# Gated recurrence: the score block of a chunk's own keys takes all 128 keys of the tile as its stationary operand

## The chip, the cores and the metric

One core of a Trainium2 chip runs the whole program. The time of a kernel is the device time of one execution in microseconds (us); the kernel before took 1293.85 us, the median of 3 runs.

## The reference

The program is one inference step of a two-layer trunk (width 1024) over 128 context tokens and 1024 latent tokens. The even layer joins a bidirectional gated linear recurrence (4 heads, state 128x128) and a neighbourhood attention; the odd layer is a convolution with a gated recurrence of its own. Only the first recurrence is touched. Per head and direction it is computed in chunks:

```python
b = jnp.cumsum(log_f, axis=3)
q_dec = q * jnp.exp(b)
k_inv = k * jnp.exp(-b)
att = jnp.where(lower, jnp.einsum('bhntd,bhnsd->bhnts', q_dec, k_inv), 0.0)
o_intra = jnp.einsum('bhnts,bhnsv->bhntv', att, v)
...
o_inter = jnp.einsum('bhntd,nbhdv->bhntv', q_dec, s_prev)
```

So each chunk needs a block of scores: its queries against its own keys, masked to a triangle. The second direction runs over the flipped sequence.

## The kernel before

All 1152 tokens lie on the free axis in three pieces of 384 columns (c = 0, 1, 2), features on the 128 partitions. A piece holds three tiles of 128 tokens (r = 0, 1, 2), and a tile two chunks of 64 tokens (e = 0, 1). Direction d = 0 runs forward, d = 1 backward.

The function att(h, d) makes the scores of one head in one direction, all in float32. For each piece it takes one bank of PSUM (ps_a; there are two) and fills, for each tile, a square of 128 keys (partitions) by 128 queries (columns). The 64 query columns of a chunk are one matmul:

- The chunk that comes first in the direction (e == f, line 561) sees only keys of its own. The stationary operand is the 64 columns of those keys in HK (named kp in the trace), the output is a block of 64 partitions by 64 columns.
- The chunk that comes second (line 563) sees both chunks' keys. Its stationary operand is all 128 key columns of the tile in HA (named s in the trace), the output is 128 partitions by 64 columns.

The moving operand q is 128x64 in both (named eb for d = 0 and q for d = 1). For d = 0 line 561 comes ahead of line 563 in each tile, for d = 1 behind it, so the two lines take turns. A float32 matmul is issued as two pairs of a weight load and a matmul, so line 561 has 4 heads x 2 directions x 9 tiles = 72 matmuls and 144 instructions of each kind, and so has line 563; a line-561 matmul with its line-563 neighbour is called a pair here, and there are 72.

The scores leave PSUM by three reads for each piece: two masked copies on DVE (line 566, the two diagonal blocks of 64x64) and one copy on ACT (line 569, recorded at line 77 of the helper act: the block of the second chunk's queries with the first chunk's keys). The fourth block, the first chunk's queries with the second chunk's keys, is read by nobody.

Around att, ew1, ew1x and ew2 prepare a head (scans on DVE, exponentials on ACT, products on DVE and POOL), ew3 and ktrans follow it, kv makes the chunk states, o_chunk the outputs (bank ps_o, of which there is one) and o_trans transposes them. These are put on an agenda and run between the units of the big input projections: unit_f (lines 316 to 318) and unit_v (lines 339 to 341), 24 matmuls each. Weights are loaded on the SP queue, split into a high part on ACT (wh, line 77) and a low part on POOL (wl, line 186), one to three blocks ahead. The framework orders each engine's instructions by priority, operands and free buffers when the program is built, and sets the semaphores; on the chip each engine goes through its list in that order.

Of the kernel before, what the change touches and what calls it, by code (L numbers as in the profile page):

```python
# [33 lines left out]
def trunk_kernel(ctx: ExitStack, tc: tile.TileContext, x, wm0, wm, bmr, wfe, wv, woe, wfo, woo, rgw, sm, st0,  # L34
# [7 lines left out]
    V, A, G, PE = nc.vector, nc.scalar, nc.gpsimd, nc.tensor  # L42
# [4 lines left out]
    def slab(name, shape=(128, T), dt=F32):  # L47
        return sp.tile(list(shape), dt, name=name, tag="slab")
# [3 lines left out]
    def psum(tag, shape=(128, 512)):  # L52
        return pp.tile(list(shape), F32, name="ps_" + tag, tag=tag, bufs=PB[tag])
# [15 lines left out]
    def act(out, in_, func, **kw):  # L69

        if func in SETS and chain["set"] not in SETS[func]:
            ld = mybir.InstLoadActFuncSet(name=nc.get_next_instruction_name(), engine=nc.scalar.engine,
                                          act_func_set_id=SETS[func][0], ins=[], outs=[])
            nc.scalar.add_instruction(ld)
            after(ld, chain["users"])
            chain.update(load=ld.name, set=SETS[func][0], users=[])
        i = A.activation(out, in_, func, **kw)  # L77
        if func in SETS:
            after(i.ins, [chain["load"]])
            chain["users"].append(i.ins.name)  # L80
        return i
# [238 lines left out]
    def unit_f(i, c, tag=None):  # L320

        ucount[0] += 1
        ps = psum(tag or ("o" if i >= IFO and ucount[0] % 4 == 0 else "mm"))
        o = ps[:, :CW]
        for k in range(8):
            mm_f(o, i, c, k)
        return o
# [30 lines left out]
    HQ, HS, HK = {}, {}, {}  # L358
# [49 lines left out]
    for jj in range(4):  # L408
        pm = psum("a")
        for kk in range(4):  # L410
            for k in (2 * kk, 2 * kk + 1):
                for b in range(4):
                    PE.matmul(pm[32 * b:32 * b + 32, 0:128], condS[:, k, :],
                              rows[jj, kk][:, (k % 2) * 512 + b * 128:(k % 2) * 512 + (b + 1) * 128],
                              start=(k == 0), stop=(k == 7), skip_group_check=True)
# [126 lines left out]
    def qt(h, d, c, r, n=128):  # L542
        if d == 0:
            return HC[h, 0][:, c * CW + r * n:c * CW + (r + 1) * n]
        return HQ[h, c][:, r * n:(r + 1) * n]

    def att(h, d):

        t = slab("at", (128, 9, 128))
        HAT[h, d] = t  # L550
        f, a = d, HA[h, d]
        fs, gs = slice(64 * f, 64 * f + 64), slice(64 - 64 * f, 128 - 64 * f)
        for c in range(3):
            pa = psum("a")
            for r in range(3):
                o = pa[:, r * 128:(r + 1) * 128]
                z = slice(r * 128, (r + 1) * 128)
                for e in range(2):
                    q = qt(h, d, c, 2 * r + e, 64)
                    if e == f:  # L560
                        PE.matmul(o[fs, fs], HK[h, d, c][:, z][:, fs], q, start=True, stop=True)
                    else:
                        PE.matmul(o[:, gs], a[:, c * CW + r * 128:c * CW + (r + 1) * 128], q, start=True, stop=True)
            p3 = pa[:, :CW].rearrange("p (t s) -> p t s", s=128)
            for zs in (fs, gs):
                V.tensor_tensor(t[zs, 3 * c:3 * c + 3, zs].bitcast(I32), p3[zs, :, zs].bitcast(I32),
                                am[zs, None, 128 * d + zs.start:128 * d + zs.stop].to_broadcast([64, 3, 64]),
                                OP.bitwise_and)
            act(HAT[h, 0][fs, 3 * c:3 * c + 3, gs], p3[fs, :, gs], AF.Copy)
        for c in range(3):  # L570
            HK.pop((h, d, c))
        if d == 1:
            t0 = HAT[h, 0]
            t1 = HAT.pop((h, 1))
            for zs in (fs, gs):
                G.tensor_tensor(t0[zs, :, zs], t0[zs, :, zs], t1[zs, :, zs], OP.add)
# [92 lines left out]
    def head(h, first=None):  # L669
        i0 = IH[h]  # L670
        U = clock["u"] + (15 if h == 0 else 12)
        at(U, s0_load, h)
        for d in range(2):
            at(U + STEP[0], ew1, h, d)
        for d in range(2):
            at(U + STEP[1], ew1x, h, d)
        for d in range(2):
            for n, f in enumerate((ew2, att, ew3, ktrans)):
                at(U + STEP[2 + n], f, h, d)
            at(U + STEP[6], kv, h, d, 0)  # L680
            at(U + STEP[7], kv, h, d, 1)
        for c in range(3):
            at(U + STEP[8 + c], o_chunk, h, c)
            at(U + STEP[8 + c], o_done, h, c)
            at(U + STEP[11 + c], o_trans, h, c)
        for n in range(4):
            w_get(i0 + n, 0, 2)
            for c in range((2 if n < 3 else 1) if first else 0, 3):
                o = unit_f(i0 + n, c)
                with tc.high_priority(200):  # L690
                    head_evac(h, n, c, o)
                tick()
            split.pop(i0 + n)
# [226 lines left out]
    for p in range(4):  # L920
        for n in range(3):
# [5 lines left out]
            for c in range(3):  # L927
                o = unit_f(i, c, (None, "a", "b")[c] if p == 3 and n == 2 else None)
                tick()
                z = slice(c * CW, (c + 1) * CW)  # L930
# [85 lines left out]
    for t in range(9):  # L1016
# [10 lines left out]
        if t in HT1:  # L1027
            c = HT1.index(t)
# [188 lines left out]
    for pos in range(max(ev) + 1):  # L1217
# [6 lines left out]
        n, c = seq[pos]  # L1224
# [147 lines left out]
```

## Time and profile before

| | us |
|---|---|
| median of 3 runs | 1293.85 |
| the 3 runs | 1293.85, 1298.67, 1292.9 |
| the profiled execution | 1299.53 |
| its span, first to last instruction | 1297.5 |

The span is what the views of the trace are measured in. PE is TensorE's matmuls and PEld its weight loads, which run beside matmuls; DVE is VectorE, ACT ScalarE, POOL GpSimd, SP the queue that issues transfers.

### The profile page before, as it was taken

The page shows a single profiled execution, that of the slowest core. Times are in us where ns is not written, and L with a number is a line of the kernel's source. Part 1 is how long each engine was busy: PE and PEld are TensorE (multiplying, and loading weights), DVE is VectorE, ACT ScalarE, POOL GpSimd, SP SyncE. Part 2 cuts the span into 40 slices and gives each one's busy share as a digit, 9 for nine tenths or more (in the row PEclk, how much of TensorE's full clock was granted, in tenths as well). Part 3 has the DMA queues.
Part 4 walks back from the last instruction along what each step waited for, and adds up shares of the span by engine and source line. Part 5 has one row for each costly group of instructions (what it writes and reads, how often), then busy time and mean ns, then how long its engine had stood idle before and what let it go on. Part 6 is the DMA issues. An engine that isn't in the chain of part 4 may idle for free.

```text
span 1297.5 us, 19173 instructions
## 1 busy us (share of the span) xinstructions
PE 1218.8 (94%) x7536; PEld 1085.6 (84%) x7536; DVE 692.1 (53%) x1422; ACT 539.2 (42%) x1065; POOL 380.4 (29%) x271
## 2 busy tenths in 40 slices
PE   4999999999999999998999999999989899988998
PEld 3889998999998997888956667888989799987886
DVE  5547028314546200000078996655668978799844
ACT  3435134323343211111146674324376676776311
POOL 0143032421504111102160420026355664644000
PEclk9999999999997999999979999999999999999999
DMA  9510100111010356513430225223001101112332
GB/s 346 190 34 21 33 17 26 34 53 37 17 40 19 126 181 216 201 62 101 127 137 2 97 82 179 98 98 130 17 26 41 41 25 42 41 33 87 142 130 82
DMA packets 41909, 110.45 MB, mean 85 GB/s; under 512 B 4180, under 2 KB 14804, under 8 KB 41820
## 3 DMA queue, kind: packets, MB, share of 16 engines
q1 hardware_dynamic: 41820, 109.24, 24.8%
q8 instruction: 59, 0.97, 0.3%
q14 instruction: 30, 0.25, 0.1%
HBM read 96.61 MB, written 12.61 MB: 84 GB/s over the span
## 4 chain that ended last, share of the span: by engine, by line
PE 55%; DVE 13%; ACT 6%; issue 4%; DMA 3%; POOL 2%; SPq 1%; POOLq 0%; ACTq 0%; DVEq 0%
PE ps_mm L316 8%; PE ps_mm L318 7%; PE ps_mm L317 7%; PE ps_mm L994 5%; PE ps_mm L995 5%; PE ps_mm L993 5%; DMA wraw<-in_wfe_dram 3%; DVE yT L1136 2%; DVE P L856 2%; DVE xc L1060 2%; ACT P L77 1%; PE ps_mm L339 1%; PE ps_mm L341 1%; PE ps_mm L340 1%; PE ps_a L221 1%
## 5 line engine op out<-in xcount | busy, mean ns | idle before, releaser
L316 PE MATMUL ps_mm<-hTh,wh 128*128 128x384 f32 x936 | 321.0, 347 | 15.8 <-ACT xp L77 4.8
L317 PE MATMUL ps_mm<-hTl,wh 128*128 128x384 f32 x936 | 320.4, 343 | 2.3 <-DVE hTl L307 1.7
L318 PE MATMUL ps_mm<-hTh,wl 128*128 128x384 f32 x936 | 320.3, 342 | 1.0 <-POOL wl L186 1.0
L186 POOL TENSOR_TENSOR wl<-wraw,wh 128x1024 fp32r<-128x1024 f32 x50 | 127.1, 2546 | 287.5 <-ACT wh L77 253.9
L316 PEld LDWEIGHTS ps_mm<-hTh,wh 128*128 128x128 f32 x936 | 178.3, 192 | 32.4 <-ACT kq L77 10.0
L317 PEld LDWEIGHTS ps_mm<-hTl,wh 128*128 128x128 f32 x936 | 178.7, 191 | 4.8 <-DVE hTl L307 3.3
L318 PEld LDWEIGHTS ps_mm<-hTh,wl 128*128 128x128 f32 x936 | 178.7, 191 | 2.0 <-POOL wl L186 1.7
L994 PE MATMUL ps_mm<-wl,yh 128*128 128x512 f32 (+1 forms) x288 | 113.6, 395 | 4.6 <-DVE wl L186 4.6
L995 PE MATMUL ps_mm<-wh,yl 128*128 128x512 f32 (+1 forms) x288 | 112.5, 391 | 0.0
L993 PE MATMUL ps_mm<-wh,yh 128*128 128x512 f32 (+1 forms) x288 | 112.4, 392 | 0.0
L77 ACT ACTIVATE wh<-wraw 128x1024 fp32r<-128x1024 f32 x68 | 71.3, 1057 | 71.2 <-DMA wraw<-in_wfe_dram 42.9
L262 POOL TENSOR_TENSOR ss<-ss,nhalf 128x1 f32<-128x1 f32 x27 | 15.2, 564 | 244.5 <-DVE ss L261 186.1
L339 PE MATMUL ps_mm<-wh,hTh 128*128 128x256 f32 x288 | 83.5, 290 | 2.4 <-ACT va L77 2.4
L341 PE MATMUL ps_mm<-wh,hTl 128*128 128x256 f32 x288 | 81.9, 284 | 0.0
L340 PE MATMUL ps_mm<-wl,hTh 128*128 128x256 f32 x288 | 81.7, 284 | 0.0
L77 ACT ACTIVATE res<-xt 128x512 f32<-128x512 f32 (+1 forms) x37 | 22.9, 620 | 123.5 <-DVE xt L1003 115.6
L994 PEld LDWEIGHTS ps_mm<-wl,yh 128*128 128x128 f32 x288 | 54.5, 189 | 19.3 <-DVE wl L186 7.6
L821 POOL TENSOR_TENSOR nbm<-mkt,bT 128x384 f32<-128x384 f32 x42 | 45.7, 1109 | 84.3 <-DMA bT<-in_bias_dram 40.8
L365 DVE SCALAR_TENSOR_TENSOR yT<-yT,ps_mm 128x384 f32<-128x384 f32 x10 | 5.5, 553 | 115.2 <-ACT yT L77 115.2
L993 PEld LDWEIGHTS ps_mm<-wh,yh 128*128 128x128 f32 x288 | 54.4, 189 | 12.3 <-issue 0.3
L995 PEld LDWEIGHTS ps_mm<-wh,yl 128*128 128x128 f32 x288 | 54.6, 189 | 11.4
L1127 POOL TENSOR_TENSOR yT<-yT,rt 128x384 f32<-128x384 f32 x42 | 56.4, 1371 | 23.4 <-ACT rt L77 19.3
(260 smaller groups left out, 2493.2 us busy)
## 6 DMA issues: line engine op xcount, KB each, us to landing
wm<-in_wm_dram SPq DMA_DIRECT2D x48, 512.0 KB
wraw<-in_wfe_dram SPq DMA_DIRECT2D x28, 512.0 KB
xt<-in_x_dram SPq DMA_DIRECT2D x18, 512.0 KB
bT<-in_bias_dram SPq DMA_DIRECT2D x48, 192.0 KB
wraw<-in_wfo_dram SPq DMA_DIRECT2D x16, 512.0 KB
x_d<-xt SPq DMA_DIRECT2D x9, 512.0 KB
xt<-x_d SPq DMA_DIRECT2D x9, 512.0 KB
out_dram<-xt SPq DMA_DIRECT2D x18, 256.0 KB
```

Source lines behind the costliest of these rows:

```text
L77: i = A.activation(out, in_, func, **kw)
L186: (lo_eng or G).tensor_tensor(lo, r, hi.bitcast(F32), OP.subtract)
L316: PE.matmul(o, w1, hh, start=(k == 0), stop=False)
L317: PE.matmul(o, w1, hl, start=False, stop=False)
L318: PE.matmul(o, w2, hh, start=False, stop=(k == 7))
L339: PE.matmul(o, hh, w1, start=(k == 0), stop=False)
L340: PE.matmul(o, hh, w2, start=False, stop=False)
L341: PE.matmul(o, hl, w1, start=False, stop=(k == 7))
L993: PE.matmul(o[:, :q - p], yh[:, z], wh[:, p:q], start=(k == 0), stop=False)
L994: PE.matmul(o[:, :q - p], yh[:, z], wl[:, p:q], start=False, stop=False)
L995: PE.matmul(o[:, :q - p], yl[:, z], wh[:, p:q], start=False, stop=(k == 7))
L1127: G.tensor_tensor(us[c], us[c], r[:, c * CW:(c + 1) * CW], OP.mult)
```

## The change

In the first chunk's matmul the stationary operand becomes all 128 key columns of the tile instead of its own 64, and the output all 128 partitions instead of 64. The 64 query columns, the moving operand and the reads are as they were. The block of the first chunk's queries with the second chunk's keys is now written; nobody reads it.

```diff
@@ -558,7 +559,7 @@
                 for e in range(2):
                     q = qt(h, d, c, 2 * r + e, 64)
                     if e == f:
-                        PE.matmul(o[fs, fs], HK[h, d, c][:, z][:, fs], q, start=True, stop=True)
+                        PE.matmul(o[:, fs], HK[h, d, c][:, z], q, start=True, stop=True)
                     else:
                         PE.matmul(o[:, gs], a[:, c * CW + r * 128:c * CW + (r + 1) * 128], q, start=True, stop=True)
```

A blank line is added above, so line 561 of the kernel before is line 562 of the kernel after.

## Rows read from the trace of the kernel before

**Rows 1.** The page: busy time and share by engine, and the chain that ended last.
```profile
PE 1218.8 (94%) x7536; PEld 1085.6 (84%) x7536; DVE 692.1 (53%) x1422; ACT 539.2 (42%) x1065; POOL 380.4 (29%) x271
PE 55%; DVE 13%; ACT 6%; issue 4%; DMA 3%; POOL 2%; SPq 1%; POOLq 0%; ACTq 0%; DVEq 0%
```

**Rows 2.** Windows over the third head's att, and the fourth's behind 400.77 us.
```profile
core 0: us, PE busy (x) PEld busy (x) DVE busy (x) ACT busy (x) POOL busy (x), PEclk, DMA share, GB/s
330.30:343.20 12.90, 12.90 (x83) 10.27 (x82) 6.94 (x19) 2.60 (x7) 3.59 (x5) 1.00 0.15 42
400.77:412.90 12.13, 12.13 (x61) 10.58 (x61) 4.35 (x10) 1.86 (x9) 2.62 (x3) 0.65 0.01 1
```

**Rows 3.** The chain through the fourth head's preparation: start us, us, what.
```profile
376.22 0.49 ACT yT L77
...
400.77 0.53 PE ps_o L627 x2
```

**Rows 4.** PE's longest wait from 150 to 420 us: us in total, times, longest.
```profile
PE ps_o L627 <- DVE on L638: 3.6, 2, 3.2
```

**Rows 5.** ACT's timeline ahead of that wait, which ended at 217.31 us.
```profile
194.79 0.49 ACT L77 ACTIVATE yT<-ps_mm 128x384 f32<-128x384 f32 x1 [2.31 <-PE ps_mm L318]
```

**Rows 6.** Timeline, start of the first head's att: start us, us, engine, line.
```profile
155.42 0.33 PE L318 MATMUL ps_mm<-hTh,wl 128*128 128x384 f32 x1
155.68 0.19 PEld L561 LDWEIGHTS ps_a<-eb,kp 128*64 128x64 f32 x2 [0.24 <-issue]
155.68 0.33 PE L561 MATMUL ps_a<-eb,kp 128*64 128x64 f32 x2
155.94 0.43 PE L563 MATMUL ps_a<-eb,s 128*128 128x64 f32 x2
156.30 0.33 PE L561 MATMUL ps_a<-eb,kp 128*64 128x64 f32 x2
```

**Rows 7.** The chain at full clock: a pair, then float32 matmuls of full width.
```profile
221.19 0.36 PE ps_a L563 x2
221.55 0.26 PE ps_a L561 x2
...
238.14 0.45 PE ps_o L630 x4
...
257.39 1.79 PE ps_b L610 x16
```

**Rows 8.** Line 561's and line 563's weight loads, d = 0: ns min/median/max.
```profile
L561 PEld LDWEIGHTS ps_a<-eb,kp x72: 132/134/136, 155.7 to 399.5; 128*64 128x64 f32 x72
L563 PEld LDWEIGHTS ps_a<-eb,s x72: 186/188/189, 155.9 to 399.8; 128*128 128x128 f32 x72
```

**Rows 9.** Windows behind 400.77 us of line 561 alone, then of line 563.
```profile
400.77:412.90 12.13, 3.25 (x18) 2.01 (x18) 0.65 0.01 1
...
400.77:412.90 12.13, 4.08 (x16) 3.04 (x16) 0.65 0.01 1
```

**Rows 10.** The chain at half clock: a pair, then full-width float32 matmuls.
```profile
410.60 0.41 PE ps_a L561 x2
411.00 0.62 PE ps_a L563 x2
...
415.06 0.85 PE ps_o L630 x4
```

**Rows 11.** DVE's and ACT's timelines: the reads of one piece.
```profile
157.66 0.72 DVE L566 TENSOR_TENSOR at<-ps_a,am 64x192 int32<-64x192 int32 x2 [27.48 <-PE ps_a L563]
158.48 0.32 ACT L77 ACTIVATE at<-ps_a 64x192 f32<-64x192 f32 x1 [1.82 <-DVE at L566]
```

**Rows 12.** The chain behind the modulation rows, where the next weights are waited for.
```profile
568.46 1.07 PE ps_a L221 x8
...
572.71 11.12 DMA wraw<-in_wfe_dram
```

**Rows 13.** A window behind the fourth head's att; columns as in rows 2.
```profile
407.90:418.20 10.30, 10.30 (x48) 9.53 (x47) 4.73 (x7) 0.95 (x4) 4.92 (x3) 0.50 0.01 2
```

## The prediction

> **What bounds the kernel now.** I read the page first, for which engine carries the end: PE is busy for 94% of the span, and the chain that ended last runs over PE for more than half of it; no other engine comes near [rows 1]. An average says nothing of the stage that is changed, so the windows over the calls of att come next. Three of the four heads look alike; the third stands for them. PE is busy for every one of its 12.90 us, while DVE has 6.94 us of work and ACT 2.60 us [rows 2]. There, time that PE saves is time that the stage saves.
>
> The fourth head is different. Ahead of 400.77 us the chain leaves PE at 376.22 us and runs through ACT, DVE and POOL, the preparation of that head, until line 627 starts on PE at 400.77 us [rows 3]. What PE saves between the two is waited out at line 627. Behind 400.77 us PE is full again (12.13 of 12.13 us) [rows 2].
>
> The first head needs one more look, because the chain as printed begins only behind it. PE has no idle time from the first att until the longest wait of this stretch: 3.2 us, for DVE's line 638 [rows 4]. If that wait hung on something with a time of its own, the first head's gain would be swallowed by it. ACT's timeline says that it doesn't: the work behind the wait (table load, logarithms, scans, exponentials) begins with an evacuation at 194.79 us for which ACT had itself waited 2.31 us on PE [rows 5]. That is behind the first att, so everything from there on moves with PE.
>
> **The change, part by part.** No instruction is removed, added or moved; 144 weight loads and 144 matmuls of line 561 change their width. What does the narrow width cost? In the timeline of the first att, a line-561 group starts at 155.68 us, the line-563 group behind it at 155.94, and the next line-561 group at 156.30 us: 0.62 us for a pair, or 0.155 us for each of its four instructions [rows 6]. The chain says the same, 0.36 + 0.26 us [rows 7]. And where line 561 follows a 128*128 matmul, the weight load is not started beside it: PEld sits idle for 0.24 us, with nothing to wait for (issue) [rows 6].
>
> Now a stretch of float32 matmuls that all have the form 128*128, each with another stationary operand: 16 of line 610 take 1.79 us, 4 of line 630 take 0.45 us [rows 7]. That is 0.112 us each, and the next load runs beside the matmul. They move 128 columns, twice those of att, so att's can hardly need more. The difference between 0.155 and 0.112 is what I take the change of form to cost: 4 x 0.043 = 0.17 us in a pair, which crosses the border between the forms twice, so 0.09 us a crossing.
>
> Behind the change all four instructions have the one form. Pair: 4 x 0.112 = 0.45 us instead of 0.62, which gives 0.17 us. The two bounds of this: the wider load is longer, 188 ns against 134 [rows 8], so if the pause stayed, a pair would become 2 x 0.054 = 0.11 us longer; and if att's 64 columns made the matmuls shorter than line 610's, more than 0.17 us would be gained, but the loads of 128 columns stay, so I set no more than 0.02 us on that. I take 0.17 us, since rows 7 differ from att after the change in the moving columns alone.
>
> At half clock the price is the same: 0.41 + 0.62 = 1.03 us for a pair, against 0.85 us for four instructions of line 630, which gives 0.18 us [rows 10].
>
> The sum. A head has 18 pairs (9 tiles, 2 directions). Three heads on PE's path: 54 x 0.17 = 9.2 us. Of the fourth, 18 instructions of line 561 and 16 of line 563 lie behind 400.77 us [rows 9]; that is 8.5 pairs, 1.4 us (0.18 each would make it 1.5). Together 10.6 us. Entries add a little: L318 to line 561 takes 0.26 us [rows 6], and by the 0.09 us a crossing some 0.17 would do; about six entries give 0.5 us. Total 11 us, with no term against it.
>
> What must keep pace: the reads. A piece is three pairs, 1.87 us of PE now and 1.35 us then. Its reads take 0.72 us on DVE, then 0.32 us on ACT, and the last ends 158.80 - 157.66 = 1.14 us after the first begins [rows 11]. With two banks, a piece may start when the reads of the last but one are over, so 1.14 us must fit under 1.35 us. It does, by 0.2 us, and units' matmuls stand between some pieces. If DVE is late by another operation (its work in the third head's att is 6.94 us, which would have to fit in 12.9 - 3.1 = 9.8 us [rows 2]), PE stalls. I cost this at nothing; without the cover, 0.2 us for each of 18 pieces on the path, 3.6 us.
>
> Is the gain kept later? The nearest place where a transfer ends last is behind the modulation rows, 11.12 us for weights [rows 12]. That load is issued after DVE has read PE's last modulation product, which ends at 569.53 us, so it starts earlier by as much as PE does. No transfer with a start of its own is left to absorb it.
>
> **A rule that speaks against it.** The 54 ns between a load of 64 columns and one of 128 are in rows 8. The Trainium skill, in "TensorE: Matmul & The Clock Gate", section "LDWEIGHTS (loading the stationary operand)", says that a load takes its number of columns over 1.2 GHz, so the change adds an estimated 53 ns to each load. The trace agrees with the size; by this rule alone the change would be a loss of 125 x 0.053 = 6.6 us on the path, an estimate from that page.
>
> **The rivals.**
> *Slower: the loads set the pace and the pause stays.* If the 0.155 us is not the change of width but something else that line 561 and line 563 share (the 64 moving columns, the taking of turns between two sources), each load is longer by 0.054 us. On the path are 54 + 8.5 = 62.5 pairs, 125 loads: 6.8 us, to about 1300.6 us. For it: the loads really are longer [rows 8]. Against it: line 630 takes turns between sources too and has no pause, and PEld's idle 0.24 us stands at the border of the two forms [rows 6, 7]. It decides from a pair of more than 0.62 us.
>
> *The change of width costs nothing.* The pace is then whatever it was, and the longer load is hidden: 1293.9 us. Against it are the same rows.
>
> *The reads become the bound.* DVE's work in att and the two banks hold PE up by 0.2 us a piece: 11 - 3.6 = 7.4 us are left, 1286.5 us; at twice that stall, 1290. For it: the slack is only 0.2 us. Against it: ACT waits 1.82 us for DVE there and DVE for PE [rows 11].
>
> *The gain is taken back elsewhere.* The order of instructions is fixed when the program is built, and a matmul's width may shift it; or the first head's gain is lost at the 3.2 us wait [rows 4], and the fourth's at its preparation. Then only two heads count: 36 x 0.17 = 6.1 us, 1287.7 us.
>
> *More than forecast: the clock.* Behind the fourth att PE runs for 10.3 us at a granted clock of 0.50, the lower of its levels, 1.2 GHz, fully busy [rows 13]; it fell after att's matmuls, with their pauses, and two waits of PE. If a closer packed att keeps it at 2.4 GHz, the half of that, 5.1 us, comes on top: 1277.7 us. Against it: three other atts ran at full clock and left it there, so the waits may matter more.
>
> **How the numbers follow.** The profiled execution took 1299.53 us, 5.7 us over the median of the runs, with a span of 1297.5 us; the gain is in stretches that do not differ by execution, so I take it from the median: 1293.85 - 11 = 1282.8 us. Chances: the forecast 0.55, the clock on top 0.13, the reads 0.12, taken back in part 0.09, no effect 0.04, slower 0.07. From 1276 us (the clock's case with 1.5 us for the spread of executions) to 1290 us (the reads at their worst) 0.86 of this is held. A measurement tells about 0.5% here from no change, 6.5 us, that is 1287.4 us. Faster: forecast, clock, half of the reads and half of the partial case, 0.78. Same: the other halves and no effect, 0.15. Slower: 0.07.
>
> **What would show it.** In the profile after, line 562 in place of 561: its loads at some 188 ns, a pair at 0.45 us (0.22 + 0.22 in the chain), no idle time of PEld at the border to L316 to L318, and each of the first three atts 3 us shorter, with DVE's and ACT's busy time unchanged. A pair that is still at 0.62 us makes the prediction wrong at its root; PE waiting at line 562 on ACT (line 569) or DVE would show the second bank to be too late; a start of line 627 in the fourth head that isn't some 9 us earlier would show gain lost on the way; and a window of half clock that has come or gone is the clock's case.

## The result and the profile after

The kernel after took 1284.69 us, the median of 4 runs (1279.99 to 1288.07), beside 1296.26 us for the kernel before in 4 runs (1292.9 to 1312.25). The ratio is 0.9868, with a 95% interval of 0.9824 to 0.9911: 0.9 to 1.8% shorter. This ratio leaves out runs that lie over 1.5% above the fastest of their kernel, and it is not the quotient of the two medians, which is 0.9911 (11.6 us). A second comparison on another occasion gave 1283.95 us and 0.9867 (0.9825 to 0.9909). The profiled execution took 1288.07 us with a span of 1286.1 us, 11.4 us less than the span before.

The page of the kernel after, its busy times and its chain, answers to [rows 1]: 11.6 us less of PE, 6.4 us less of DVE, ACT and POOL as they were.

```profile
PE 1207.2 (94%) x7536; PEld 1083.1 (84%) x7536; DVE 685.7 (53%) x1422; ACT 540.1 (42%) x1065; POOL 381.2 (30%) x271
PE 52%; DVE 14%; ACT 6%; issue 4%; DMA 4%; POOL 2%; SPq 1%; POOLq 0%; ACTq 0%; DVEq 0%
```

The timeline of the first att, and the loads' durations (ns min/median/max), answer to [rows 6, 8]. Line 562 is line 561 of before, line 564 is line 563.

```profile
156.74 0.34 PE L318 MATMUL ps_mm<-hTh,wl 128*128 128x384 f32 x1
156.92 0.33 PE L562 MATMUL ps_a<-eb,kp 128*128 128x64 f32 x2
...
157.31 0.39 PE L562 MATMUL ps_a<-eb,kp 128*128 128x64 f32 x2
157.53 0.39 PE L564 MATMUL ps_a<-eb,s 128*128 128x64 f32 x2
157.75 0.39 PE L562 MATMUL ps_a<-eb,kp 128*128 128x64 f32 x2
...
156.74 0.36 PEld L562 LDWEIGHTS ps_a<-eb,kp 128*128 128x128 f32 x2
...
L562 PEld LDWEIGHTS ps_a<-eb,kp x72: 186/192/235, 156.7 to 392.8; 128*128 128x128 f32 x72
```

From one line-562 group to the next it is now 157.31 to 157.75 us, 0.44 us for a pair (0.22 for each group of two), where it was 0.62. The load of line 562 starts at 156.74 us together with the matmul of L318; the 0.24 us in which PEld sat idle at this border are gone. The loads themselves have become longer, 192 ns against 134.

The chain in order of time answers to [rows 3, 7, 10, 12]; the two lines from 398.85 us are at half clock.

```profile
215.94 0.77 PE ps_o L628 x2
...
219.95 0.22 PE ps_a L562 x2
220.17 0.22 PE ps_a L564 x2
...
369.77 0.49 ACT yT L77
...
394.32 0.80 PE ps_o L628 x2
...
398.85 0.43 PE ps_a L564 x2
399.28 0.43 PE ps_a L562 x2
...
556.80 1.07 PE ps_a L221 x8
...
561.04 11.06 DMA wraw<-in_wfe_dram
```

PE's waits from 150 to 420 us answer to [rows 4].

```profile
PE ps_o L628 <- DVE on L639: 3.5, 2, 3.2
PE ps_a L562 <- ACT at L77: 1.8, 1, 1.8
PE ps_a L564 <- ACT at L77: 1.0, 3, 0.4
```

At half clock a pair takes 0.43 + 0.43 us, where it took 1.03 [rows 10].

And windows behind the fourth head's preparation, and over the half clock there, answer to [rows 2, 13]: columns as there.

```profile
394.32:403.80 9.48, 9.48 (x61) 9.48 (x62) 4.68 (x12) 1.87 (x9) 2.70 (x3) 0.72 0.01 2
392.90:399.70 6.80, 6.54 (x31) 6.35 (x31) 2.42 (x5) 1.24 (x8) 2.89 (x2) 0.50 0.00 0
```

With these marks the span divides into stretches that can be set side by side (each is a difference of two starts, before then after, in us):

| stretch | before | after | difference |
|---|---|---|---|
| start to first att | 155.68 | 156.92 | +1.2 |
| first att to the second head's wait of PE | 61.63 | 59.02 | -2.6 |
| from there to the fourth head's preparation | 158.91 | 153.83 | -5.1 |
| preparation, to line 627 / 628 on PE | 24.55 | 24.55 | 0.0 |
| from there to the end of the last modulation product | 168.76 | 163.55 | -5.2 |
| the rest | 727.97 | 728.23 | +0.3 |

The first and the last row hold nothing that was changed. Between them 12.9 us are gone, 7.7 of them with the first three atts.

One stretch can be compared free of the clock: from line 627 of the second head (628 after the change) to that of the third head, with the third head's att in it. The windows are before, then after.

```profile
273.44:382.61 109.17, 109.17 (x686) 105.63 (x686) 42.66 (x91) 41.53 (x83) 28.54 (x20) 1.00 0.10 32
269.29:376.00 106.71, 106.36 (x687) 105.08 (x686) 41.61 (x91) 41.63 (x83) 28.66 (x20) 1.00 0.11 33
```

It is 2.46 us shorter, at full clock on both sides. In the two other profiles of the kernel before it takes 109.17 us again, in the other one of the kernel after 106.73.

### The profile page after: what moved, and what is told of

Same layout as the page of the kernel before. It is cut to its first block, busy times and chain, and to the rows that moved or that the text cites. A ratio compares the mean times of both kernels' runs of the same rounds, so it can differ in the third digit from the quotient of the medians.

```text
span 1286.1 us, 19174 instructions
## 1 busy us (share of the span) xinstructions
PE 1207.2 (94%) x7536; PEld 1083.1 (84%) x7536; DVE 685.7 (53%) x1422; ACT 540.1 (42%) x1065; POOL 381.2 (30%) x271
## 4 chain that ended last, share of the span: by engine, by line
PE 52%; DVE 14%; ACT 6%; issue 4%; DMA 4%; POOL 2%; SPq 1%; POOLq 0%; ACTq 0%; DVEq 0%
PE ps_mm L316 7%; PE ps_mm L318 7%; PE ps_mm L317 7%; PE ps_mm L995 5%; PE ps_mm L996 5%; PE ps_mm L994 5%; DMA wraw<-in_wfe_dram 3%; DVE yT L1137 2%; DVE xc L1061 2%; DVE P L857 2%; ACT P L77 1%; PE ps_a L221 1%; PE ps_mm L339 1%; PE ps_mm L341 1%; PE ps_mm L340 1%
## 5 line engine op out<-in xcount | busy, mean ns | idle before, releaser
L318 PE MATMUL ps_mm<-hTh,wl 128*128 128x384 f32 x936 | 319.8, 342 | 1.1 <-POOL wl L186 1.1
L318 PEld LDWEIGHTS ps_mm<-hTh,wl 128*128 128x128 f32 x936 | 178.7, 191 | 1.9 <-POOL wl L186 1.7
L996 PEld LDWEIGHTS ps_mm<-wh,yl 128*128 128x128 f32 x288 | 54.6, 189 | 11.4
```

Of the source, the lines that this page charges most:

```text
L318: PE.matmul(o, w2, hh, start=False, stop=(k == 7))
L996: PE.matmul(o[:, :q - p], yl[:, z], wh[:, p:q], start=False, stop=(k == 7))
```

## The experiments

The prediction had one price, 0.17 us a pair, and one reason, the change of form. Three questions were put to it: is it the change of form and not the narrow form or the taking of turns; what do the longer loads cost; and do the reads hold PE up.

**The narrow matmuls kept, but grouped.** The kernel before, with the loops over e and r exchanged:

```diff
-            for r in range(3):
-                o = pa[:, r * 128:(r + 1) * 128]
...
-                for e in range(2):
+            for e in range(2):
+                for r in range(3):
+                    o = pa[:, r * 128:(r + 1) * 128]
```

> The kernel before, with its narrow first-chunk matmuls, but in each piece the three matmuls of one line are issued together and then the three of the other: the form changes 2 times in a piece instead of 6. Theory (each change of form costs 0.09 us): a piece takes 12 x 0.112 + 2 x 0.09 = 1.52 us of PE instead of 1.87, so 4 x 0.09 = 0.36 us less; over the 62.5 / 3 = 21 pieces on the path 7.5 us less than the kernel before (ratio 0.994), about two thirds of what the change gave. Rival (the taking of turns is not what costs; the narrow form is slower in itself, or the loads set the pace): a piece stays at 1.87 us, no change against the kernel before, ratio 1.000 with 0.002 to either side.

Measured: 1280.81 us, ratio to before 0.9857 (0.9824 to 0.9889). Not two thirds of the gain but all of it, with the narrow matmul untouched. The timeline of its first att:

```profile
154.51 0.56 PE L561 MATMUL ps_a<-eb,kp 128*64 128x64 f32 x6
155.00 0.88 PE L563 MATMUL ps_a<-eb,s 128*128 128x64 f32 x6
155.81 0.56 PE L561 MATMUL ps_a<-eb,kp 128*64 128x64 f32 x6
```

A piece takes 155.81 - 154.51 = 1.30 us, not the 1.52 expected. So the rival falls (the turns between forms are what costs), and the theory's two prices fall with it: something in the narrow group is faster than 0.112 us. With N for a narrow instruction, W = 0.112 for a wide one and X for a change of form, this piece is 6N + 6W + 2X = 1.30 and the piece of before 6N + 6W + 6X = 1.87. The difference gives X = 0.14 us, and then N = 0.058 us. The rows agree with both prices: the narrow group takes 155.00 - 154.51 = 0.49 us, which is 6 x 0.058 + 0.14, and the wide one 155.81 - 155.00 = 0.81 us, which is 6 x 0.112 + 0.14. The record's 0.09 us for a crossing was a net price: the longer loads had been hidden in it.

**The same grouping with the wide matmul**, to see whether turns between two stationary operands cost without a change of form:

> The kernel after, with the same grouping: three matmuls of one line, then three of the other, all of them 128*128. Theory (changes of form): there are none to take away, so a piece stays at 12 x 0.112 = 1.34 us and the time is that of the kernel after, ratio to it 1.000 with 0.002 to either side. Rival (the turns between two stationary sources cost, whatever their form): a piece becomes shorter here too, by up to the same 0.36 us, and the time falls by up to 7 us below the kernel after.

Measured: 1281.79 us, ratio to before 0.9863 (0.9829 to 0.9897), which can't be told from the kernel after (0.9868). In its timeline,

```profile
155.27 0.83 PE L564 MATMUL ps_a<-eb,s 128*128 128x64 f32 x6
155.94 0.83 PE L562 MATMUL ps_a<-eb,kp 128*128 128x64 f32 x6
```

the second group of six starts 0.67 us behind the first, 0.112 us an instruction, as in the kernel after where the lines take turns. Turns between operands of one form cost nothing that these rows show.

**One narrow tile in each piece.** The kernel after, with this in place of its line 562; it was run twice, the second time for its profile (the profiled execution of the first took 2923.08 us and is not used; the others took 1280.21 to 1299.43):

```diff
-                        PE.matmul(o[:, fs], HK[h, d, c][:, z], q, start=True, stop=True)
+                        if r == 1:
+                            PE.matmul(o[fs, fs], HK[h, d, c][:, z][:, fs], q, start=True, stop=True)
+                        else:
+                            PE.matmul(o[:, fs], HK[h, d, c][:, z], q, start=True, stop=True)
```

> The kernel after, but the middle one of a piece's three tiles keeps the narrow first-chunk matmul. Theory (0.09 us for each change of form): 2 changes in each piece come back, 0.18 us a piece, 24 pieces 4.3 us of PE and 21 of them on the path, so about 3.7 us of the gain are lost, ratio to the kernel before about 0.990 where the change gave 0.987. Rival (all or nothing: a single narrow matmul spoils the whole piece, or the gain comes from the block of scores that is now written): the gain is lost wholly (1.000) or not at all (0.987).

> The kernel with one narrow first-chunk matmul in each piece once more, for a profile of it. Theory (0.14 us a change of form, 0.054 us less for each of two narrow loads): a tile with the narrow matmul takes 0.62 us and the other two 0.45 each, 1.51 us a piece, 0.17 us over the kernel after; 21 pieces 3.6 us, ratio to the kernel after 1.003. Rival (all or nothing): 1.000 or 1.009.

Measured: 1287.15 us, ratio to before 0.9904 (0.9867 to 0.994), and 1285.63 us, 0.9892 (0.9845 to 0.9939). Both lie between all and nothing, but the intervals overlap with the kernel after's; the timeline is what decides:

```profile
156.27 0.39 PE L567 MATMUL ps_a<-eb,s 128*128 128x64 f32 x2
156.59 0.33 PE L563 MATMUL ps_a<-eb,kp 128*64 128x64 f32 x2
156.84 0.43 PE L567 MATMUL ps_a<-eb,s 128*128 128x64 f32 x2
157.12 0.39 PE L565 MATMUL ps_a<-eb,kp 128*128 128x64 f32 x2
157.34 0.39 PE L567 MATMUL ps_a<-eb,s 128*128 128x64 f32 x2
157.56 0.39 PE L565 MATMUL ps_a<-eb,kp 128*128 128x64 f32 x2
```

Line 563 is the narrow matmul here. The three groups from 156.27 to 157.12 us, with the narrow one in their middle, take 0.85 us; the two wide ones from 157.12 to 157.56 us take 0.44, 0.22 each, so three of them would take 0.67. The narrow tile costs 0.18 us, as the theory had it (0.17), and its neighbours are as fast as ever: not all or nothing.

**Nothing but narrow matmuls.** The kernel before, with the second chunk's matmul split in two:

```diff
-                        PE.matmul(o[:, gs], a[:, c * CW + r * 128:c * CW + (r + 1) * 128], q, start=True, stop=True)
+                        ar = a[:, c * CW + r * 128:c * CW + (r + 1) * 128]
+                        PE.matmul(o[fs, gs], ar[:, fs], q, start=True, stop=True)
+                        PE.matmul(o[gs, gs], ar[:, gs], q, start=True, stop=True)
```

> The kernel before, but the second chunk's matmul is split into two narrow ones (its first chunk's keys, then its own keys, 64 columns each), so att has the narrow form alone and the order is pair by pair. Theory as the trace of the grouped narrow kernel now has it (a change of form costs 0.14 us, a load of 64 columns sets a pace of 0.058 us and one of 128 columns 0.112 us): a pair is 6 x 0.058 = 0.35 us with no change of form inside it, against 0.62 in the kernel before and 0.45 in the kernel after; 62.5 pairs on the path give 17 us less than before and 6 us less than after, so long as the reads (1.14 us a piece against 1.05 us of PE) keep up. Rival (going from one half of the columns to the other is a change of form too): two such changes in a pair, 0.35 + 0.28 = 0.63 us, the time of the kernel before. Theory of the record (0.09 us for a change, loads cost nothing, pace 0.11): 6 x 0.11 = 0.66 us, no faster than before.

Measured: 1277.75 us, ratio to before 0.9826 (0.9786 to 0.9866), the fastest of all kernels run. Its six runs lie between 1274.41 and 1279.01 us, those of the kernel after beside it between 1278.33 and 1284.71; the medians differ by 6.2 us. The timeline shows a thing that no theory had:

```profile
155.26 0.22 PE L561 MATMUL ps_a<-eb,kp 128*64 128x64 f32 x1
155.27 0.27 PE L565 MATMUL ps_a<-eb,s 128*64 128x64 f32 x1
155.32 0.22 PE L561 MATMUL ps_a<-eb,kp 128*64 128x64 f32 x1
155.38 0.22 PE L565 MATMUL ps_a<-eb,s 128*64 128x64 f32 x1
155.38 0.28 PE L564 MATMUL ps_a<-eb,s 128*64 128x64 f32 x2
155.50 0.22 PE L561 MATMUL ps_a<-eb,kp 128*64 128x64 f32 x1
```

Line 561 and line 564 write one half of the partitions, line 565 the other, and line 565 starts 0.01 us behind line 561, not after it. A pair takes 155.50 - 155.26 = 0.24 us for its six instructions: the two halves run side by side, and the pace is that of the four loads of one half, 4 x 0.058. Neither the 0.35 us expected nor the rival's 0.63 us came. The first experiment's 0.058 us is seen directly in two of them (155.26 to 155.32). That line 565 goes to the other half of the partitions and back costs nothing here, so it is the width and not the half that makes a change of form.

The gain over the kernel after is 6 us and not 62.5 x 0.21 = 13 us. The larger part of the rest is the price of the theory itself, at a place that the expectation left out: a piece is still entered from a unit's 128*128 matmul and left to one. From 150 to 425 us PE changes form 38 times in this kernel, 144 times in the kernel before and not once in the kernel after; 34 of the 38 lie outside the fourth head's preparation, and at the first experiment's 0.14 us they cost 4.8 us. The end of the first piece, and PE's waits from 150 to 420 us:

```profile
156.31 0.28 PE L564 MATMUL ps_a<-eb,s 128*64 128x64 f32 x2
156.52 0.45 PE L316 MATMUL ps_mm<-hTh,wh 128*128 128x384 f32 x1
156.81 0.34 PE L317 MATMUL ps_mm<-hTl,wh 128*128 128x384 f32 x1
...
PE ps_a L561 <- ACT at L77: 2.7, 2, 1.8
PE ps_a L564 <- ACT at L77: 1.7, 2, 1.4
```

Two narrow instructions and a unit matmul take 0.12 + 0.17 us among their like, and 156.81 - 156.31 = 0.50 us here. The reads are the smaller part: outside the preparation, which covers the wait of 1.8 us, PE waits 2.6 us for them, 1.0 in the kernel after. Together that is 6.4 of the missing 7 us (an estimate, since each price is taken from another place).

**Grouped, with every second piece turned**, so that equal forms meet:

```diff
-            for e in range(2):
+            for e in ((0, 1), (1, 0))[c % 2]:
```

> The grouped narrow kernel, but every second piece issues its two groups in the other order, so that neighbouring pieces meet with the same form: where no unit's matmul stands between two pieces, one more change of form goes. The grouped kernel has 16 changes from the wide to the narrow line without a unit between them. Theory (0.14 us each): at most 16 x 0.14 = 2.2 us of PE less, some of it paid back where a piece now ends narrow ahead of a unit, so 0 to 2 us less than the grouped narrow kernel (ratio to it 0.998 to 1.000). Rival (it is how often the lines take turns, not the form): the same small change, so this run is about the size alone.

Measured: 1279.46 us, ratio to before 0.9848 (0.9798 to 0.9898), 1.3 us under the grouped kernel's median of another comparison, which says nothing. Two wide groups now do meet without a pause, but the piece behind them ends narrow, ahead of a unit, so that from 150 to 425 us PE changes form 46 times, where the grouped kernel has 48:

```profile
156.21 1.55 PE L563 MATMUL ps_a<-eb,s 128*128 128x64 f32 x12
157.69 0.56 PE L561 MATMUL ps_a<-eb,kp 128*64 128x64 f32 x6
158.18 0.44 PE L316 MATMUL ps_mm<-hTh,wh 128*128 128x384 f32 x1
```

**One read for a piece.** Here every block is written, so the two masked copies on DVE and the copy on ACT can be one:

```diff
-            for zs in (fs, gs):
-                V.tensor_tensor(t[zs, 3 * c:3 * c + 3, zs].bitcast(I32), p3[zs, :, zs].bitcast(I32),
-                                am[zs, None, 128 * d + zs.start:128 * d + zs.stop].to_broadcast([64, 3, 64]),
-                                OP.bitwise_and)
-            act(HAT[h, 0][fs, 3 * c:3 * c + 3, gs], p3[fs, :, gs], AF.Copy)
+            V.tensor_tensor(t[:, 3 * c:3 * c + 3, :].bitcast(I32), p3.bitcast(I32),
+                            am[:, None, 128 * d:128 * d + 128].to_broadcast([128, 3, 128]), OP.bitwise_and)
...
-            for zs in (fs, gs):
-                G.tensor_tensor(t0[zs, :, zs], t0[zs, :, zs], t1[zs, :, zs], OP.add)
+            G.tensor_tensor(t0, t0, t1, OP.add)
```

> The kernel after, but with every score block written, a piece leaves PSUM by one masked read of 128 partitions x 384 columns on DVE, in place of two masked copies on DVE and one copy on ACT; the mask already holds zeros for the block that is not wanted, and the sum over the two directions on POOL takes the whole square, once instead of twice. Theory that the reads are not the bound in the kernel after: PE's waits for them are 2.8 us there, 1.8 of them under the preparation of the fourth head, so at most 1 to 2 us are gained (ratio to the kernel after 0.998 to 1.000). Rival (the reads hold PE up through the order in which the matmuls had to be put): more than 4 us are gained (0.997 or less).

Measured: 1290.9 us, ratio to before 0.9928 (0.9895 to 0.9961): nothing gained over the kernel after (0.9868), rather some 7 us lost. PE's waits from 150 to 420 us, and the one read (ns min/median/max):

```profile
PE ps_a L562 <- DVE at L566: 2.1, 1, 2.1
PE ps_a L564 <- DVE at L566: 0.5, 2, 0.2
...
L566 DVE TENSOR_TENSOR at<-ps_a,am x24: 543/557/558, 156.0 to 411.4; 128x384 int32<-128x384 int32 x24
```

Neither the theory's 0 to 2 us nor the rival's 4 us came. PE waits 2.6 us for reads, as against 2.8 us, though a piece's reads fell from 1.14 to 0.56 us; outside the preparation it is 0.5 against 1.0 us. So shorter reads have little to give here, but what they give the experiment can't show, since something else took 7 us. What that is was not settled. The profile is of an execution of 1302.83 us, 12 us over the median; in it the granted clock was half for 23.9 us from 212.4 us on, over the second head's att, which is not so in the two profiles of the kernel after. The other runs have no profile, but their mean granted clock hints at the same: 0.970 over all eleven, 0.977 over the six of the kernel after that are told of next.

**The kernel after and the kernel before once more**, the first for its time beside the others, the second twice for its profile, because the fourth head's stretch had lost more (5.2 us) than its 8.5 pairs explain (1.5 us).

> The kernel after once more, beside the others on one chip, for ratios to it: 0.987 of the kernel before, 0.982 to 0.991.

> The kernel before once more, for a second profile. Theory that the half clock behind the fourth att belongs to the kernel (its att with the pauses): between the fourth head's first line-627 matmul and the last modulation product there are again some 13 us at half clock, and that stretch takes 168 to 169 us. Rival (chance of the execution): 3 to 7 us at half clock as in the kernel after, and 164 to 166 us.

> A third profile of the kernel before, with the same expectations as the second: 13 us at half clock in that stretch by the theory, 3 to 7 us by the rival.

Measured: 1283.95 us for the kernel after, ratio 0.9867 (0.9825 to 0.9909); 1313.87 and 1298.95 us for the kernel before. In the fourth stretch the theory fell: it took 164.7 and 162.6 us, at a mean granted clock of 0.99 and 1.00. But the half clock was there, in other places. A window over the first att in the third profile (it starts at 157.80 us), columns as in [rows 2]:

```profile
161.50:182.00 20.50, 20.50 (x75) 17.36 (x75) 7.22 (x15) 2.86 (x7) 7.55 (x5) 0.50 0.00 0
```

And in the second profile, over the first and the second att (they start at 155.93 and 228.96 us):

```profile
159.10:179.60 20.50, 20.50 (x76) 17.24 (x76) 7.24 (x15) 2.69 (x6) 6.63 (x4) 0.50 0.00 0
227.40:254.70 27.30, 27.30 (x115) 22.86 (x114) 12.60 (x26) 3.28 (x14) 8.04 (x7) 0.50 0.00 1
```

PE is busy for all of it. In the first att of both, the clock falls to 1.2 GHz about two pieces behind the start, with no wait of PE ahead of it since 150 us; in the second att of the second profile it falls before the att, 1.3 us behind the end of a wait of 3.2 us. The stretch from the first att to the second head's wait then took 70.1 us in both, against 61.6.

## Why the prediction was right

**What bounds the kernel.** Right. PE's path carried the gain through, the preparation of the fourth head took 24.55 us before and after, and the weights behind the modulation rows were issued earlier with PE (11.12 and 11.06 us to land).

**The price of a pair.** Right in sum, wrong in its parts. A pair went from 0.62 to 0.44 us as forecast (0.45), and at half clock from 1.03 to 0.86 (0.85). But the step "0.17 us in a pair, which crosses the border twice, so 0.09 us a crossing" took the longer loads for free. They are not: the two crossings cost 2 x 0.14 = 0.28 us, and the two loads give back 2 x 0.054 = 0.11 us. The rival in which the loads cost 0.054 us each was right about the loads; it was wrong only in that the pause stays. That the net came out is no luck, since it was the difference of two rows; but the split was a guess, and an experiment planned on it (the grouped kernel) missed by 0.22 us a piece. The Trainium skill, in "TensorE: Matmul & The Clock Gate", section "LDWEIGHTS (loading the stationary operand)", gives a load its columns over 1.2 GHz, an estimated 0.053 and 0.107 us for 64 and 128 columns; the paces of 0.058 and 0.112 us at full clock are near that, the 0.21 us for each instruction of 0.43 + 0.43 us at half clock are not. The skill's "TensorEngine Tiling (Array Packing)", section "Key Properties", says that a change of tiling mode drains the engine, without a price. The trace agrees in so far as the load behind line 318's matmul starts 0.26 us after it where the form changes [rows 6], and together with it where it doesn't (156.74 us); the price here was 0.14 us. That the two forms are two such modes no run shows.

**The entries.** L318 to line 562 takes 0.18 us instead of 0.26, the 0.09 us forecast.

**The reads.** They were costed at nothing and took about 1.6 us. Two things came together that the prediction had set aside. It had said that no instruction is moved, but at 87 of the 7536 places of PE's list another line now stands: in the first head, two of the four unit matmuls that stood ahead of the last two pieces (lines 316 and 317, 164.23 and 164.41 us before) stand behind them now, and no longer cover the read. And a read came late: DVE had a product to finish before its own read, and ACT's copy, for which PE waited, comes behind that:

```profile
161.71 2.12 POOL L583 TENSOR_TENSOR s<-s,ex 128x1152 f32<-128x1152 f32 x1 [30.75 <-PE ps_a L564]
162.35 1.69 DVE L587 TENSOR_TENSOR eb<-eb,ex 128x192 f32<-128x192 f32 x1
165.34 0.41 PE L564 MATMUL ps_a<-q,s 128*128 128x64 f32 x2 [0.36 <-ACT at L77]
```

The product took 1.69 us beside POOL's, and 0.36 us in the median. The same stands in the second and the third head (224.90 and 331.86 us). PE's three waits are 1.0 us together. From start to start they cost more: the unit matmul ahead of this one starts at 164.57 us, 0.77 us earlier, where 0.17 us is usual, so 0.6 us are lost here, 0.4 and 0.6 in the other two heads. The wait of 1.8 us lies under the fourth head's preparation, where it costs nothing. The rival of the reads had 3.6 us, and the rival of the gain taken back named the shift of the order; both came in part. DVE's busy time was to stay and fell by 6.4 us: the products of line 586 on q took 1.51 us in the median before, most of them beside POOL's, and take 0.34 now.

**The sum.** For three heads 9.2 us and some 0.5 of entries were forecast; the stretches give 7.7. The sign "each of the first three atts 3 us shorter" did not quite come: from the first att matmul to the first unit matmul that has the same work ahead of it in both (155.68 to 168.40 us before, 156.92 to 167.11 after, in the first head) they are 2.5, 2.6 and 2.3 us shorter. The reads' 1.6 us are most of what is missing. At full clock the third head's stretch shows the same: 3.1 us forecast, 2.46 measured, 0.6 for the read. So line 628 of the fourth head starts 6.4 us earlier, not 9 (7.7 from the first att).

For the fourth head 1.4 us were forecast and 5.2 came. Of that stretch the kernel before spent 13.6 us at half clock (3.4 from 401.1 us, 10.2 from 407.9), the kernel after 5.4 (394.32 to 399.70). A pair takes 0.86 us at half clock and 0.44 at full, so about half of such time is lost, and the clock makes some 4 of the 5.2 us (an estimate from these figures) and the change about 1. That the sum of 11 us came out at 11.4 us of the spans is thus partly luck: the change itself gave about 9, the clock's 4 came on top, and 1.2 us went at a start that the change doesn't touch.

**The clock.** The fourth head's surplus is what this rival had forecast. Its window was read wrongly, though: the 10.3 us of [rows 13] do not lie behind the fourth att but begin in it, at 407.9 us, and its last matmuls, at 410.60 us [rows 10], are at half clock already. They are gone, and 6.8 us stand at 392.9 us instead. But the experiment shows that the place is chance. What may belong to the kernel before is that its atts are more open to the half clock. From the first att to the fourth head's line 627 the mean granted clock was 0.99, 0.90 and 0.96 in its three profiles, 0.99 and 1.00 in the two of the kernel after, and 0.99 or 1.00 in the grouped narrow, grouped wide, turned, all-narrow and one-narrow-tile kernels. The one-read kernel, which has no changes of form in att, is the exception with 0.93. So many changes of form and the half clock were seen together, but the pauses were not shown to be its cause. The second and the third profile are also from another chip than the other experiments.

The spread of the kernel before goes with the clock. In the comparison beside the grouped kernels, on one chip, its 22 runs lie between 1289.48 us, at a mean granted clock of 0.981, and 1314.32 us, at 0.955; those of the kernel after lie between 1278.33 and 1288.07 us. So the ratio of 0.9868, some 17 us, holds more than the change of form. At one clock less is left: of these runs the four at 0.973 or 0.974 took 1295.1 us on average, and the three of the kernel after at that clock 1285.2, a difference of 10 us (11.7 us between 0.972 and 0.975, over eight runs of both later comparisons and four). The forecast of 11 us for the change is near that; as a ratio, 0.9915, it lies just outside the measured interval.

## What to carry to other kernels

Matmuls whose stationary operands differ in width, taking turns on TensorE, paid 0.14 us at each turn here (float32, 64 moving columns, full clock): bring them to one form, or put those of one form together. Count the turns at both ends of a group too, against the work that stands around it. A narrow stationary operand is not waste in itself; where all matmuls of a stretch are narrow and write to different halves of the partitions, they were the fastest form here. Split a net price into its parts before planning on a part of it, and compare a stretch at one granted clock before a small difference of whole runs is put down to a change.

## What was not expected of the hardware

- Float32 matmuls of 64 stationary columns that write to different halves of the partitions ran side by side: six instructions in 0.24 us, where six in a row at 0.058 us would take 0.35. The Trainium skill has it that tiles operate independently ("TensorEngine Tiling (Array Packing)", "Key Properties"), and the trace agrees.
- With loads and matmuls of one form, the pace of float32 instructions with 64 moving columns went by the stationary columns: 0.058 us for 64, 0.112 us for 128. The moving columns did not set it: line 610, with 128 of them, has the same 0.112 us [rows 7].
- The granted clock was half for 20.5 and 27.3 us while PE was busy all the time, over atts with changes of form; in a kernel without any in att it was half for 23.9 us.
- A DVE product of 128x192 elements took 1.69 us beside a POOL product and 0.36 us in the median. No experiment was made of it.
